# Where the block sums of the down projection's weights are made: 44 sums moved out of the SSD into the SSD output product and the mixing product

## The chip, the core and the metric

The kernel runs on one core of a Trainium2 chip. The metric is the time of one execution on the device, in microseconds (us). The engines are TensorE (PE; PEld are its weight loads), VectorE (DVE), ScalarE (ACT), GpSimd (POOL) and SyncE (SP), which here only issues DMA transfers. Each engine works through its own queue in order; an instruction that waits holds up what stands behind it.

## What is computed

A decoder layer over 1024 tokens of width 1024: two token mixers side by side (a Mamba-2 state-space mixer, SSD, and differential attention), merged by gates, followed by a gated feed-forward network with a convolution. Everything is float32. Cut to what matters:

```python
y_ssd = ssd_branch(z, xbc, dt_raw, ...)
y_att = diff_attention_branch(q, k, v, ...)
gate_ssd, gate_att = jnp.split(jax.nn.sigmoid(gates), 2, axis=-1)
merged = gate_ssd * (y_ssd @ w_ssd_o) + gate_att * (y_att @ w_attn_o)
mix = merged @ w_out
x = x + g1 * rms_norm(mix, post_norm1_w)
h2 = rms_norm(x, pre_norm2_w) * (1.0 + sc2) + sh2
u = causal_dwconv(h2 @ w_up, conv_ffn_w, conv_ffn_b)
u_gate, u_val = jnp.split(u, 2, axis=-1)
f = (jax.nn.gelu(u_gate, approximate=True) * u_val) @ w_down
x = x + g2 * rms_norm(f, post_norm2_w)
```

`w_down` is 2816 x 1024.

## The kernel before

**Products.** A float32 product is made of three passes in a faster format: each operand is split into a high part (a copy on ACT that rounds) and a low part (the difference, on DVE; helper `split`, L94 and L95), and high x high, high x low and low x high are summed in PSUM. The stages run one after another on PE: gates and convolved inputs, z, SSD, SSD output product, attention, merging, mixing product, up projection, down projection.

**The down projection** is computed with seven block products instead of eight (a Strassen-Winograd scheme), so it needs sums of the quarters of `w_down`. With KF = 11 blocks of rows k in each half, block k has the quarters b11, b12 (rows k) and b21, b22 (rows k + 11), each 128 x 512. Four sums per block are wanted: t1 = b12 - b11, t2 = b22 - t1, t3 = b22 - b12, t4 = b21 - t2. They depend on weights alone, so they can be made at any time before the down projection. They are made on DVE and stored in two DRAM tensors `wtd["12"]` and `wtd["34"]`, from which the down projection later loads them.

**Where they are made before.** In the SSD. `down_load` (L781) loads block k into one of two pairs of 512 KB buffers `wdr`; the generator `down_sums` (L786 to L794) makes one sum per turn into two extra buffers `wds`, and SP stores them, 512 KB for each two sums. The loop over u = 0 to 15 (8 chunks of 128 tokens, 2 groups of 8 heads) calls `sum_dn` at four places in each step, so that the 44 sums are spread over the steps u = 0 to 11 (none at 7).

**One step of the SSD.** `chunk_in(u + 1)` turns the next chunk's inputs on PE (px), copies them on ACT (xtk, L1070) and scales them on DVE (xd, L1073) and POOL; `chunk_decay` makes the decays M on ACT; `chunk_mask` multiplies them by the mask on DVE (L1092); `chunk_out(u)` forms po, the product of the state of before with C (L1099), which DVE reads into tt (L1100), and py, the product within the chunk (L1103), which DVE adds to y (L1105); `chunk_state(u)` forms the new state pst (L1117). po and pst use the one PSUM bank `wc` in turns. Between these, `fill` feeds PE with groups of three products of the attention's v (L1021 to L1023), whose weights are replaced once, at u = 7 (L1008 on ACT, L1009 on DVE, `fetch_v` on SP). The orders of PE, DVE, ACT and SP are as written here.

**The SSD output product** (j = 0 to 7) multiplies the turned SSD output by `w_ssd_o`: 48 products per step into one of two PSUM pairs, an evacuation with the gate on DVE (mout, L1324), a store of it on SP (msd, L1328). `fetch_seq(j + 6)` loads weights two steps ahead of their split, `split_seq(j + 5)` splits them one step ahead of use. At j = 0 the last block of q and k is rotated and stored (`rope`, `store_qk`), at j = 3 and 4 `load_qk` loads the q and k of the first heads of the attention. The order of SP is as written here too. The attention's first weights (w_q_raw, L1362; split at L1377 and L1374) and v tiles are loaded in this stretch as well, where the scheduler puts them.

**The mixing product** (i = 0 to 7, rows of 128 tokens) multiplies the merged mixers by `w_out` into two PSUM banks per row. `mix_square` (L1880) takes a row's squares on ACT; `mix_end(i)` ends the row, in this order on DVE: a sum of squares (L1884), a power on POOL (L1885), scaling and residual for two halves (L1895, L1896), their squares on ACT (L1897), the x1 store on SP (L1898), again L1884 and L1885, and the scaling L1900. `mix_end(i - 1)` is emitted within row i after its first quarter of products. Rows 2 and up take four PSUM banks in turns, so row i + 2 needs those of row i. In rows 5 and 6 `first_half` turns the finished rows 0 to 3 on PE (L1909) for the up projection, eight units through two PSUM banks, with two or three evacuations each on ACT (L1913, L1914, L1916) and a low part on DVE (L1917). PE, DVE, ACT and POOL run in the order written here; the scheduler orders SP.

**POOL's stores.** In the merging, `early_sums` (L1672 to L1678) already makes such sums, in place, for the up projection's first weights, and POOL issues their stores.

**Slots.** Buffers of 4 KB per partition come from a list of 43 (`Slots`): `get` takes the first free one, `put` appends it. Whoever gets a slot waits for its last user.

Of the kernel before, what the change touches and what calls it, by code (L numbers as in the profile page):

```python
# [11 lines left out]
F32 = mybir.dt.float32  # L12
F32R = mybir.dt.float32r
AF = mybir.ActivationFunctionType
ALU = mybir.AluOpType
AX = mybir.AxisListType

P = 128
D = 1024
S = 1024  # L20
HALF = 512
# [41 lines left out]
def kernel(ctx: ExitStack, tc: tile.TileContext, a: dict, out: bass.AP, dbg=None):  # L63
    nc = tc.nc
    V, A, G, T, SP = nc.vector, nc.scalar, nc.gpsimd, nc.tensor, nc.sync
# [15 lines left out]
    def ps_mm(name):  # L81
        return pmm.tile([P, 2, HALF], F32, tag="mm", name=name, bufs=2)
# [37 lines left out]
    def block_half(ps, w, x, half):  # L120
        mm3(ps, [((w[0][:, k, :], w[1][:, k, :]), (x[k][half][:, 0, :], x[k][half][:, 1, :])) for k in range(KD)])
# [302 lines left out]
    KF = NFF // 2  # L424
# [347 lines left out]
        SL.put(*evs_x, *cgv[(m - 1) % 2])  # L772


    dn_ops = deque()

    def down_load(k):
        if k < KF:
            for i in range(2):
                r0 = (k + KF * i) * P  # L780
                SP.dma_start(wdr[k % 2][i].rearrange("p h c -> p (h c)"), a["w_down"][r0 : r0 + P, :])  # L781

    def down_sums(k):
        (b11, b12), (b21, b22) = [(t[:, 0, :], t[:, 1, :]) for t in wdr[k % 2]]
        t1, t2, t3, t4 = wds[0][:, 0, :], wds[0][:, 1, :], wds[1][:, 0, :], wds[1][:, 1, :]
        V.tensor_tensor(t1, b12, b11, op=ALU.subtract)  # L786
        yield
        V.tensor_tensor(t2, b22, t1, op=ALU.subtract)
        SP.dma_start(wtd["12"][:, k, :, :], wds[0])
        yield  # L790
        V.tensor_tensor(t3, b22, b12, op=ALU.subtract)
        yield
        V.tensor_tensor(t4, b21, t2, op=ALU.subtract)
        SP.dma_start(wtd["34"][:, k, :, :], wds[1])  # L794
        down_load(k + 2)
        yield

    def all_sums():
        for k in range(KF):
            yield from down_sums(k)  # L800


    sm1 = SL.get("sm1", F32, (P, 8, 8, NH))
    sm2 = SL.get("sm2", F32, (P, 1024))
# [359 lines left out]
    for u in range(3):  # L1164
        load_decay(u)
    load_z(0)
    wdr = [[SL.get(f"wdr{i}{j}", F32, (P, 2, HALF)) for j in range(2)] for i in range(2)]
    wds = [SL.get(f"wds{i}", F32, (P, 2, HALF)) for i in range(2)]
    sums_dn = all_sums()

    def sum_dn(u, n):
        if u == 7 or (u == 8 and n < 2):
            return
        for _ in range(2 if u < 2 and n == 3 else 1):
            next(sums_dn, None)

    with tc.manual_schedule(engines={EN.PE, EN.DVE, EN.Activation, EN.SP}):
        for k in range(2):
            down_load(k)
        chunk_in(0)  # L1180
        fill(2)
        chunk_decay(0)
        chunk_mask(0, 0)
        chunk_mask(0, 1)
        lamt = const("lamt", [P, 2, 64])
        lams = const("lams", [P, 2])
        nlam = const("nlam", [P, 1])
        rl = rows[:, R_LAM : R_LAM + 256].rearrange("p (a b d) -> p a b d", a=2, b=2)
        V.tensor_tensor(lamt, rl[:, :, 0, :], rl[:, :, 1, :], op=ALU.mult)
        V.reduce_sum(lams, lamt, axis=AX.X)  # L1190
        A.activation(lams, lams, AF.Exp)
        V.tensor_tensor(nlam, lams[:, 1:2], lams[:, 0:1], op=ALU.subtract)
        V.tensor_scalar(nlam, nlam, -LAM_INIT, None, op0=ALU.add)
        subw = const("subw", [P, 1])
        V.tensor_scalar(subw, vec[:, V_SUB : V_SUB + 1], 1.0 - LAM_INIT, None, op0=ALU.mult)
        fill(4)
        for u in range(16):
            nxt = u + 1 < 16
            if u > 0:
                load_decay(u + 2)  # L1200
            if nxt:
                chunk_in(u + 1)
            fill(2)
            run_bg(2)
            sum_dn(u, 0)
            if nxt:
                chunk_decay(u + 1)
            run_bg(1)
            sum_dn(u, 1)
            if nxt:  # L1210
                chunk_mask(u + 1, 0)
            fill(2)
            chunk_out(u, (lambda: chunk_mask(u + 1, 1)) if nxt else (lambda: None))
            fill(3)
            run_bg(3)
            sum_dn(u, 2)
            chunk_state(u)
            fill(1 if u % 3 else 0)
            run_bg(1)
            sum_dn(u, 3)  # L1220
            if u % 2 == 1:
                chunk_norm(u // 2)
            if u == 11:
                assert next(sums_dn, None) is None
                SL.put(*wdr[0], *wdr[1], *wds)
                yr = [SL.get(f"yr{i}") for i in range(4)]
                ropc, rops = SL.get("ropc"), SL.get("rops")
                SP.dma_start(ropc, a["ropc"])
                SP.dma_start(rops, a["rops"])
                fetch_seq(0)  # L1230
                fetch_seq(1)
            elif u == 12:
                load_y(0)
        fill(16 * KD)
        run_bg(len(bg))
# [31 lines left out]
    def split_seq(n):  # L1267
        if n < len(seq):
            raw = seq_w[n]
            seq_w[n] = [wp.tile([P, KD, P], F32R, tag=f"w{x_}", name=f"{seq[n][0]}{seq[n][1]}_{x_}", bufs=4) for x_ in ("hi", "lo")]  # L1270
            split(*seq_w[n], raw)
# [11 lines left out]
    with tc.manual_schedule(engines={EN.PE, EN.DVE, EN.Activation, EN.SP}):  # L1283
        split_seq(0)
        old = None
        for n in range(4):
            fetch_seq(n + 2)
            ps = ps_mm(f"{seq[n][0]}p{seq[n][1]}")
            for half in range(2):
                block_half(ps[:, half, :], seq_w[n], hT, half)  # L1290
                if half == 0:
                    if old is not None:
                        rope(*old)
                    split_seq(n + 1)
                for k in turns[n][half]:
                    turn_y(k, n // 2)
                if n == 1 and half == 0:
                    load_y(1)
                if half == 0 and old is not None:
                    store_qk(*old[:2], hi, lo)  # L1300
            old = (*seq[n], ps)
        SL.put(*yr)


        gths = [SL.get(f"gth{i}") for i in range(2)]
        mouts = [SL.get(f"mout{i}") for i in range(2)]
        SP.dma_start(gths[0], gsd[0])
        for j in range(8):
            gth, mout = gths[j % 2], mouts[j % 2]
            fetch_seq(j + 6)  # L1310
            if j + 1 < 8:
                SP.dma_start(gths[(j + 1) % 2], gsd[j + 1])
            ps = ps_mm(f"so{j}")
            block_half(ps[:, 0, :], seq_w[j + 4], yT, 0)
            if j == 0:
                rope(*old)
                store_qk(*old[:2], hi, lo)
                SL.put(hi, lo, ropc, rops, qf, sw)
                qst, kst, klo = [[[SL.get(f"{n}0_{s}", F32R) for s in range(2)]] for n in ("qst", "kst", "klo")]
            split_seq(j + 5)  # L1320
            block_half(ps[:, 1, :], seq_w[j + 4], yT, 1)
            for half in range(2):
                hsl = slice(half * HALF, (half + 1) * HALF)
                V.scalar_tensor_tensor(mout[:, hsl], gth[:, hsl], 1.0, ps[:, half, :], op0=ALU.add, op1=ALU.mult)  # L1324
            if j in (3, 4):
                s = j - 3
                load_qk(s, qst[0][s], kst[0][s], klo[0][s])
            SP.dma_start(msd[j], mout)  # L1328
    SL.put(*gths, *mouts)
# [528 lines left out]
    rsm2 = const("rsm2", [P, 8])  # L1858
    pms = [None] * 8

    def load_res(i):
        SP.dma_start(xr[i], a["x"][i * P : (i + 1) * P, :])
        if i < 2:
            pms[i] = [(ps_wa, (ps_wb, ps_wc)[i])[ch](f"mix{i}_{ch}") for ch in range(2)]
        else:
            pms[i] = [ps_m(2 * (i % 2) + ch, f"mix{i}_{ch}") for ch in range(2)]
# [81 lines left out]
    with tc.manual_schedule(engines={EN.PE, EN.DVE, EN.Activation, EN.Pool}):  # L1948
        k0, k1 = range(KH), range(KH, KD)
        units = list(range(KD))  # L1950
        for i in range(8):
            if i == 0:
                for j in range(2):
                    load_res(j)
                for j in range(2):
                    mix_mms(j, 1, range(KD))
                for j in range(2):
                    mix_square(j, 1)
                mix_mms(0, 0, range(KD))
                mix_square(0, 0)  # L1960
                continue
            if i == 1:
                mix_mms(1, 0, k0)
                mix_end(0)
                mix_mms(1, 0, k1)
                mix_square(1, 0)
                continue
# [3 lines left out]
            for n, (ch, ks) in enumerate(((0, k0), (0, k1), (1, k0), (1, k1))):  # L1971
# [9 lines left out]
                    r1s = [SL.get(f"hr1{i}", F32, (P, 2, HALF)) for i in range(2)]  # L1981
                if n == 1:
                    mix_square(i, 0)
                if i in (5, 6):
                    for _ in range(1 + (i == 5 and n == 3)):
                        if units:
                            first_half(units.pop(0))
# [425 lines left out]
```

## Time and profile before

| | |
|---|---|
| median of 3 runs | 1841.29 us (1841.15 to 1841.5) |
| the profiled execution | 1841.71 us, its span 1839.9 us |
| mean granted clock of TensorE | 0.997 |
| PE busy | 1805.2 us, 98% |
| DVE busy | 1295.0 us, 70% |
| ACT busy | 896.3 us, 49% |
| POOL busy | 143.6 us, 8% |
| DMA | 334.66 MB, mean 182 GB/s |

The span runs from the first to the last instruction; the execution's time has the start and the end around it as well. Busy is the time in which an engine works on an instruction; the time in which it waits is not counted. In a row of the groups or of a timeline stand the line, the engine, the operation, out<-in by the program's names with their shapes, and in brackets how long the engine had been idle before it and what ended that. In the down stretch of the kernel nothing but loads of `wtd` (first at 1661.0 us of the span) uses the sums.

### The profile page before, as it was taken

The numbers are of one execution on the slowest core, as the hardware profiler recorded it, in microseconds if no ns is written. First come the engines' busy times: TensorE is split into PE (matmuls) and PEld (weight loads), VectorE is DVE, ScalarE is ACT, GpSimd is POOL, SyncE is SP. The second block draws the span as 40 slices with busy tenths as digits, with TensorE's granted clock in tenths as the row PEclk, the third lists the DMA queues.
The fourth block names the chain that finished last, engine by engine and source line by source line (L and its number), as shares of the span: only waits on it lengthen the run. The fifth ranks groups of instructions, "written<-read, shape, count | busy, mean of one in ns | idle before, by whom it ended". The sixth has DMA issues, their size and how long they took to land.

```text
span 1839.9 us, 24115 instructions
## 1 busy us (share of the span) xinstructions
PE 1805.2 (98%) x8787; PEld 1507.6 (82%) x8787; DVE 1295.0 (70%) x1978; ACT 896.3 (49%) x1744; POOL 143.6 (8%) x128
## 2 busy tenths in 40 slices
PE   7999999998999999999999999999999999999998
PEld 4888899876888888888888888888888888888887
DVE  7888877698753267767667563487998888876545
ACT  7554532545531046565567232565545454465532
POOL 0000000256420000000000100000000000000001
PEclk9999999999999999999999999999999999999999
DMA  9475367798747746676724764122333223379744
GB/s 374 180 246 172 99 206 265 263 358 303 281 128 208 228 124 172 173 192 159 192 87 160 240 209 157 57 87 100 112 109 109 103 97 109 108 233 309 247 154 162
DMA packets 133672, 334.66 MB, mean 182 GB/s; under 512 B 15009, under 2 KB 39345, under 8 KB 133554
## 3 DMA queue, kind: packets, MB, share of 16 engines
q1 hardware_dynamic: 132594, 329.98, 54.6%
q0 software_dynamic: 960, 3.15, 0.5%
q8 instruction: 69, 1.13, 0.3%
q14 instruction: 49, 0.40, 0.1%
HBM read 237.83 MB, written 95.23 MB: 181 GB/s over the span
## 4 chain that ended last, share of the span: by engine, by line
PE 65%; DVE 5%; ACT 3%; issue 1%; DMA 1%; POOL 0%; DVEq 0%; POOLq 0%; ACTq 0%
PE upx L1815 4%; PE upx L1816 4%; PE upx L1814 4%; PE o L1508 3%; PE upy L1815 2%; PE upy L1814 2%; PE upy L1816 2%; PE dx L2178 2%; PE dx L2179 2%; PE dx L2177 2%; PE at L1495 2%; PE dy L2178 2%; PE dy L2179 2%; PE dy L2177 2%; PE sc L1450 2%; PE ao L118 2%
## 5 line engine op out<-in xcount | busy, mean ns | idle before, releaser
L1814 PE MATMUL upx<-t,wu_t 128*128 128x512 f32 x264 | 103.2, 391 | 0.5 <-DVE cv L2242 0.4
L1815 PE MATMUL upx<-t,wu_t 128*128 128x512 f32 x264 | 102.8, 390 | 0.2 <-DVE t L1932 0.2
L1816 PE MATMUL upx<-t,wu_t 128*128 128x512 f32 x264 | 102.7, 389 | 0.0
L1788 ACT ACTIVATE wu_t<-sab 128x512 fp32r<-128x512 f32 x57 | 34.2, 627 | 128.3 <-DVE sab L1805 128.3
L1496 ACT COPY aT<-at 128x512 f32<-128x512 f32 (+2 forms) x96 | 46.1, 480 | 95.9 <-PE at L1495 95.9
L95 DVE TENSOR_TENSOR g_lo<-gst,g_hi 128x1024 fp32r<-128x1024 f32 (+1 forms) x42 | 47.6, 1135 | 50.7 <-ACT g_hi L94 50.6
L1508 PEld LDWEIGHTS o<-vt,aT 128*128 128x128 f32 x576 | 75.3, 191 | 9.2 <-ACT aT L1496 4.6
L1508 PE MATMUL o<-vt,aT 128*128 128x128 f32 x576 | 80.8, 276 | 0.4 <-ACT aT L1496 0.2
L94 ACT ACTIVATE g_hi<-gst 128x1024 fp32r<-128x1024 f32 (+1 forms) x42 | 41.6, 990 | 66.4 <-DMA gst<-gld_s 37.6
L1469 DVE TENSOR_REDUCE nmx<-sc 128x1 f32<-128x640 f32 (+3 forms) x64 | 65.6, 1025 | 2.2
L1449 PE MATMUL sc<-kst,qst 128*128 128x512 f32 (+2 forms) x192 | 63.7, 340 | 0.0
L1450 PE MATMUL sc<-klo,qst 128*128 128x512 f32 (+2 forms) x192 | 63.2, 346 | 0.0
L1832 DVE SCALAR_TENSOR_TENSOR ug<-cg,vec,ug 128x1023 f32<-128x1023 f32 (+1 forms) x44 | 56.3, 1280 | 6.1 <-ACT ug L1831 5.3
L1814 PEld LDWEIGHTS upx<-t,wu_t 128*128 128x128 f32 x264 | 49.5, 188 | 11.7 <-DVE cv L2242 1.3
L1815 PEld LDWEIGHTS upx<-t,wu_t 128*128 128x128 f32 x264 | 49.6, 188 | 10.7 <-DVE t L1932 0.5
L1792 DVE TENSOR_TENSOR wu_t<-sab,wu_t 128x512 fp32r<-128x512 f32 x57 | 39.3, 690 | 26.6 <-ACT wu_t L1788 26.6
L1816 PEld LDWEIGHTS upx<-t,wu_t 128*128 128x128 f32 x264 | 49.6, 188 | 10.3
L1832 DVE SCALAR_TENSOR_TENSOR uv<-cv,vec,uv 128x1023 f32<-128x1023 f32 (+1 forms) x44 | 56.2, 1278 | 0.9 <-ACT uv L1831 0.9
L1485 DVE RECIPROCAL rsm<-ssum 128x2 f32<-128x2 f32 x64 | 10.6, 166 | 62.6 <-ACT p L1482 35.4
L1487 DVE SCALAR_TENSOR_TENSOR p<-p,coef,p 128x128 f32<-128x128 f32 (+3 forms) x64 | 52.4, 819 | 2.3
L2298 POOL TENSOR_TENSOR rsf<-rsf,nhalf 128x1 f32<-128x1 f32 x8 | 5.3, 656 | 624.3 <-DVE rsf L2297 624.3
L2177 PE MATMUL dx<-wdt_hi,g_hi 128*128 128x512 f32 x132 | 51.3, 389 | 0.0
(546 smaller groups left out, 5871.0 us busy)
## 6 DMA issues: line engine op xcount, KB each, us to landing
adas<-in_w_ada SPq DMA_DIRECT2D x32, 512.0 KB, 4.8
wdr<-in_w_down SPq DMA_DIRECT2D x22, 512.0 KB, 6.8
wtd<-wds SPq DMA_DIRECT2D x22, 512.0 KB, 4.4
wuf<-in_w_up SPq DMA_DIRECT2D x22, 512.0 KB, 3.5
gld_s<-gsum SPq DMA_DIRECT2D x22, 512.0 KB, 2.8
gst<-gld_s SPq DMA_DIRECT2D x20, 512.0 KB, 4.6
wdt_raw<-wtd SPq DMA_DIRECT2D x20, 512.0 KB, 4.5
wuv<-in_w_up SPq DMA_DIRECT2D x19, 512.0 KB, 3.5
```

The source lines that it names most:

```text
L1449: T.matmul(sc[:, n0:n1], qs_[s][:, tsl], ks_[s][:, n0:n1], start=True, stop=False)
L1450: T.matmul(sc[:, n0:n1], qs_[s][:, tsl], kl[s][:, n0:n1], start=False, stop=True)
L1469: V.reduce_max(nmx[:, bq, s : s + 1], sc[:, :L], axis=AX.X, negate=True)
L1487: V.scalar_tensor_tensor(pr[0][:, :L], pr[1][:, :L], coef[:, bq : bq + 1], pr[0][:, :L], op0=ALU.mult, op1=ALU.add)
L1508: T.matmul(po_of[j, grp][:, qi, :], at[:, k, :], vt[j % 2][:, kt, :], start=(kt == 0), stop=(kt == i))
L1814: T.matmul(out_, wh, xh_, start=(k == 0 and first), stop=False, skip_group_check=not first)
L1815: T.matmul(out_, wh, xl_, start=False, stop=False, skip_group_check=not first)
L1816: T.matmul(out_, wl, xh_, start=False, stop=(k == end), skip_group_check=not first)
L1832: V.scalar_tensor_tensor(u[:, d:], c_[:, : S - d], fw[:, 2 - d : 3 - d], u[:, d:], op0=ALU.mult, op1=ALU.add)
L2177: T.matmul(o, gh[:, kk, tsl], wh, start=(k == 0 and not more), stop=False, skip_group_check=more)
L2178: T.matmul(o, gh[:, kk, tsl], wl, start=False, stop=False, skip_group_check=more)
L2179: T.matmul(o, gl[:, kk, tsl], wh, start=False, stop=(k == KF - 1), skip_group_check=more)
```

## The change

The sums leave the SSD. They are made in place, so `wds` is gone: t1 takes the place of b11, t3 that of b12, t2 that of b22, t4 that of b21, in the order t1, t3, t2, t4, and each is stored by itself (256 KB). Blocks 0 to 3 (16 sums) are made in the SSD output product: two blocks are loaded at j = 0 (two more at j = 2 and 3), and at j = 1 to 4 DVE makes four sums behind the split of that step, with SP issuing the stores. `load_qk` moves from j = 3 and 4 to j = 5 and 6, since its buffers are used for the blocks. Blocks 4 to 10 (28 sums) are made in the mixing product, with three pairs of buffers and POOL issuing the stores: 4 sums after row 0's products, 4 after `mix_end(0)`, and 7, 7 and 6 in rows 2, 3 and 4, behind the `mix_end` of the row before.

```diff
-    def down_sums(k):
-        (b11, b12), (b21, b22) = [(t[:, 0, :], t[:, 1, :]) for t in wdr[k % 2]]
-        t1, t2, t3, t4 = wds[0][:, 0, :], wds[0][:, 1, :], wds[1][:, 0, :], wds[1][:, 1, :]
-        V.tensor_tensor(t1, b12, b11, op=ALU.subtract)
...
-        SP.dma_start(wtd["34"][:, k, :, :], wds[1])
-        down_load(k + 2)
...
+    KSO = 4
+
+    def down_load(t, k, i):
+        r0 = (k + KF * i) * P
+        SP.dma_start(t[i].rearrange("p h c -> p (h c)"), a["w_down"][r0 : r0 + P, :])
+
+    def down_sum(t, k, n, q):
+        (b11, b12), (b21, b22) = [(x_[:, 0, :], x_[:, 1, :]) for x_ in t]
+        o, x_, y_ = ((b11, b12, b11), (b12, b22, b12), (b22, b22, b11), (b21, b21, b22))[n]
+        V.tensor_tensor(o, x_, y_, op=ALU.subtract)
+        q.dma_start(wtd[("12", "34", "12", "34")[n]][:, k, n // 2, :], o)
...
-        for k in range(2):
-            down_load(k)
         chunk_in(0)
...
-            sum_dn(u, 0)
...
-            sum_dn(u, 1)
...
-            sum_dn(u, 2)
...
-            sum_dn(u, 3)
...
             if u == 11:
-                assert next(sums_dn, None) is None
-                SL.put(*wdr[0], *wdr[1], *wds)
...
+            if 2 <= j < KSO:
+                for i in range(2):
+                    down_load(wdr[j % 2], j, i)
...
             if j == 0:
                 rope(*old)
                 store_qk(*old[:2], hi, lo)
-                SL.put(hi, lo, ropc, rops, qf, sw)
+                SL.put(ropc, rops, qf, sw, hi, lo)
+                wdr = [[SL.get(f"wdr{k}{i}", F32, (P, 2, HALF)) for i in range(2)] for k in range(2)]
+                for k in range(2):
+                    for i in range(2):
+                        down_load(wdr[k], k, i)
+            elif j == KSO + 1:
+                SL.put(*wdr[0], *wdr[1])
                 qst, kst, klo = [[[SL.get(f"{n}0_{s}", F32R) for s in range(2)]] for n in ("qst", "kst", "klo")]
             split_seq(j + 5)
+            if 1 <= j <= KSO:
+                for n in range(4):
+                    down_sum(wdr[(j - 1) % 2], j - 1, n, SP)
...
-            if j in (3, 4):
-                s = j - 3
+            if KSO < j < KSO + 3:
+                s = j - KSO - 1
                 load_qk(s, qst[0][s], kst[0][s], klo[0][s])
...
+    wdr = [[SL.get(f"wdm{k}{i}", F32, (P, 2, HALF)) for i in range(2)] for k in range(3)]
+    dn_todo = [(k, n) for k in range(KSO, KF) for n in range(4)]
+
+    def dn_step(count):
+        for _ in range(min(count, len(dn_todo))):
+            k, n = dn_todo.pop(0)
+            t = wdr[k % 3]
+            down_sum(t, k, n, G)
+            if n > 1 and k + 3 < KF:
+                down_load(t, k + 3, n - 2)
+            elif n == 3:
+                SL.put(*t)
...
             if i == 0:
                 for j in range(2):
                     load_res(j)
+                for k in range(KSO, KSO + 3):
+                    for n in range(2):
+                        down_load(wdr[k % 3], k, n)
...
                 mix_square(0, 0)
+                dn_step(4)
                 continue
             if i == 1:
                 mix_mms(1, 0, k0)
                 mix_end(0)
+                dn_step(4)
...
                 if n == 1:
                     mix_square(i, 0)
+                if n > 0 and i < 5:
+                    dn_step(3 if n < 3 else 1)
```

More of the change, by code (lines that the diff above doesn't have):

```diff
@@ L772 @@
         SL.put(*evs_x, *cgv[(m - 1) % 2])
[L775 to L781, printed above, removed]
-    def down_sums(k):
-        (b11, b12), (b21, b22) = [(t[:, 0, :], t[:, 1, :]) for t in wdr[k % 2]]
-        t1, t2, t3, t4 = wds[0][:, 0, :], wds[0][:, 1, :], wds[1][:, 0, :], wds[1][:, 1, :]
[L786 to L793, printed above, removed]
-        SP.dma_start(wtd["34"][:, k, :, :], wds[1])
-        down_load(k + 2)
[L796 to L800, printed above, removed]
+    KSO = 4
[7 more added lines that the diff above has]
+        q.dma_start(wtd[("12", "34", "12", "34")[n]][:, k, n // 2, :], o)
     sm1 = SL.get("sm1", F32, (P, 8, 8, NH))
@@ L1166 @@
     load_z(0)
[L1167 to L1175, printed above, removed]
     with tc.manual_schedule(engines={EN.PE, EN.DVE, EN.Activation, EN.SP}):
-        for k in range(2):
-            down_load(k)
         chunk_in(0)
```

## The prediction

> **What bounds the kernel now.** I read the busy times first, then the windows of the four stretches that the change touches: the SSD, the SSD output product, and the mixing product up to its fourth and in its last rows. The columns of a window are its bounds, its length, the busy time of PE, PEld, DVE, ACT and POOL with instruction counts, the granted clock, the DMA share and GB/s.
>
> ```profile
> PE 1805.2 (98%) x8787; PEld 1507.6 (82%) x8787; DVE 1295.0 (70%) x1978; ACT 896.3 (49%) x1744; POOL 143.6 (8%) x128
> ```
>
> ```profile
> 326.00:508.00 182.00, 171.76 (x889) 137.14 (x888) 146.60 (x209) 101.21 (x260) 89.37 (x64) 0.98 0.83 298
> 553.00:642.00 89.00, 88.88 (x396) 73.42 (x395) 27.33 (x35) 12.88 (x15) 3.43 (x1) 1.00 0.73 223
> 1107.00:1163.00 56.00, 56.00 (x249) 46.37 (x248) 20.49 (x35) 14.54 (x38) 4.38 (x8) 1.00 0.31 121
> 1163.00:1200.00 37.00, 36.71 (x178) 30.21 (x177) 21.01 (x36) 25.37 (x53) 3.26 (x6) 1.00 0.18 70
> ```
>
> PE sets the end: work taken off another engine is worth only the PE idle time that it causes. In all 1839.9 - 1805.2 = 34.7 us are idle, and the SSD holds 182.00 - 171.76 = 10.24 of them, beside a DVE busy 81% of the time and DMA at 0.83. The two places that receive the sums have a full PE and much DVE time free. So the question is how much of the 10.24 comes back, and whether the new places can hide 44 sums.
>
> The waits of PE inside the SSD, with total, times and longest:
>
> ```profile
> PE pst L1117 <- DVE tt L1100: 8.3, 5, 3.6
> PE v L1021 <- ACT wv_hi L1008: 1.2, 1, 1.2
> PE v L1022 <- DVE wv_lo L1009: 0.8, 1, 0.8
> ```
>
> They make 10.3, all of it. The state product (pst) shares one PSUM bank with po, and waits until DVE has read po into tt. The timelines of DVE and of PE around the longest wait say why tt is late; the last bracket is the idle time ahead and its releaser.
>
> ```profile
> 362.32 0.69 DVE L786 TENSOR_TENSOR wds<-wdr 128x512 f32<-128x512 f32 x1 [3.33 <-DMA wtd<-wds]
> ...
> 365.59 1.53 DVE L791 TENSOR_TENSOR wds<-wdr,wdr 128x512 f32<-128x512 f32 x1
> 367.04 0.68 DVE L793 TENSOR_TENSOR wds<-wdr,wds 128x512 f32<-128x512 f32 x1
> 367.64 0.68 DVE L1092 TENSOR_TENSOR M<-M,sm 128x512 f32<-128x512 f32 x1
> 368.25 0.68 DVE L1100 TENSOR_TENSOR tt<-po,sm 128x512 f32<-128x512 f32 x1
> ```
>
> ```profile
> 369.07 2.04 PE L1117 MATMUL pst<-xdd,sm 128*128 128x512 f32 x2 [3.56 <-DVE tt L1100]
> ...
> 374.96 0.42 PE L1021 MATMUL v<-wv_hi,hT 128*128 128x512 f32 x1
> ...
> 391.80 1.10 PE L1117 MATMUL pst<-xdd,sm 128*128 128x512 f32 x2 [0.76 <-DVE tt L1100]
> ...
> 394.90 0.39 PE L1021 MATMUL v<-wv_hi,hT 128*128 128x512 f32 x1
> ```
>
> A block sum stood 3.33 us at the head of DVE's queue for its own output buffer, and two more went ahead of tt. The same 15 instructions (pst to the third v group) then took 374.96 - 369.07 = 5.89 us after the long wait, 394.90 - 391.80 = 3.10 otherwise: 2.79 us lost again, at a reduced clock (the window's 0.98).
>
> **The change part by part.**
>
> *Removed from the SSD.* 44 sums on DVE, 22 loads and 22 stores on SP. The costliest and the cheapest of the four kinds, from the groups:
>
> ```profile
> L793 DVE TENSOR_TENSOR wds<-wdr,wds 128x512 f32<-128x512 f32 x11 | 13.9, 1266 | 0.0
> ...
> L786 DVE TENSOR_TENSOR wds<-wdr 128x512 f32<-128x512 f32 x11 | 8.5, 775 | 4.3 <-DMA wtd<-wds 4.3
> ```
>
> Each step of the loop loses about four sums, 3 to 5 us of DVE. The five tt waits are at most 3.56 us each with two or more sums ahead of tt in that step, so they go: -8.3. So does the slow clock, -2.8. The last pair, 1.2 + 0.8, is a weight load (wv_raw) issued only when DVE has finished a split; that split starts earlier and the load no longer shares DMA with 23 MB of sums, so I take -1.9, with zero as the other bound. Together **-13.0**, bounds -11.1 and -13.0. Nothing next in line is near: the loop's last steps have no sums and the window shows no PE wait there.
>
> *SSD output product: 16 sums in four steps, four 512 KB loads at once, then four more, 16 stores on SP.*
>
> ```profile
> 576.29 1.28 DVE L1324 SCALAR_TENSOR_TENSOR mout<-gth,so 128x512 f32<-128x512 f32 x2 [8.48 <-PE so L118]
> 578.50 1.23 DVE L95 TENSOR_TENSOR w_ssd_o_lo<-w_ssd_o_raw,w_ssd_o_hi 128x1024 fp32r<-128x1024 f32 x1 [0.93 <-ACT w_ssd_o_hi L94]
> 587.17 1.29 DVE L1324 SCALAR_TENSOR_TENSOR mout<-gth,so 128x512 f32<-128x512 f32 x2 [7.44 <-PE so L118]
> ```
>
> ```profile
> wdr<-in_w_down SPq DMA_DIRECT2D x22, 512.0 KB, 6.8
> wtd<-wds SPq DMA_DIRECT2D x22, 512.0 KB, 4.4
> ```
>
> ```profile
> 571.29 0.38 SPq L1328 DMA_DIRECT2D msd<-mout  x1
> ```
>
> A step lasts 587.17 - 576.29 = 10.88 us and DVE idles 7.4 to 8.5 of it, so four sums (2.7 at 0.68 each) fit. The tight place is step 1: behind the first waiting sum stand the evacuation (mout) and the split of the weights for step 3, and on SP behind the stores the next weight fetch. The loads go out where this first store of mout now stands on SP, at 571.3 to 573, and the first pair lands 6.8 later (the median of such loads, from the DMA issues), near 579; sums until 582, mout 583, split 585, needed at 587. Hidden by 2 us: **0**; if the loads take 10 it costs 1.5, and never below nothing, since PE is full.
>
> *Moved: the q/k loads of the first heads, two steps later.* Their ten issues go past the loads of the attention's first weights on SP.
>
> ```profile
> 623.85 0.38 SPq L1362 DMA_DIRECT2D w_q_raw<-in_w_q  x1
> ```
>
> ```profile
> 629.83 1.16 ACT L1377 ACTIVATE w_q_hi<-w_q_raw 128x512 fp32r<-128x512 f32 x2 [12.82 <-DMA w_q_raw<-in_w_q]
> ```
>
> ```profile
> 641.37 0.39 PE L1403 MATMUL w_qp<-hT,w_q_hi 128*128 128x512 f32 x1
> ```
>
> If the w_q load slips a whole step, its split starts at 629.83 + 10.88 = 640.7; high half 0.58, low half 0.69 give 642.0, plus 0.2 of handing over, where the third product wants it at 641.8. **+0.4**, bounds 0 and 2.
>
> *Mixing product: 28 sums on DVE between the row ends (4, 4, 7, 7, 6), each with a store that POOL issues, and the loads on SP.* Each row end (mix_end) is in order on DVE with two powers on POOL and two squares on ACT between; the first-half transposes stand behind it on ACT.
>
> ```profile
> 1125.28 0.16 DVE L1884 SCALAR_TENSOR_TENSOR rsm<-ssm 128x1 f32<-128x1 f32 x1 [11.12 <-ACT tm L1880]
> ...
> 1131.27 0.15 DVE L1884 SCALAR_TENSOR_TENSOR rsm<-ssm 128x1 f32<-128x1 f32 x1
> ...
> 1141.65 0.16 DVE L1884 SCALAR_TENSOR_TENSOR rsm<-ssm 128x1 f32<-128x1 f32 x1 [4.35 <-ACT tm L1880]
> ...
> 1163.41 0.16 DVE L1884 SCALAR_TENSOR_TENSOR rsm<-ssm 128x1 f32<-128x1 f32 x1 [4.83 <-ACT tm L1880]
> ```
>
> ```profile
> 1039.71 0.69 DVE L1673 TENSOR_TENSOR ws<-ws,ws 128x512 f32<-128x512 f32 x1
> 1040.44 0.69 DVE L1674 TENSOR_TENSOR ws<-ws,ws 128x512 f32<-128x512 f32 x1
> 1041.17 0.69 DVE L1675 TENSOR_TENSOR ws<-ws 128x512 f32<-128x512 f32 x1
> 1041.45 0.75 POOL L1677 DMA_DIRECT2D wsd<-ws  x1 [27.85 <-DVE ws L1674]
> ...
> 1052.31 0.54 POOL L1677 DMA_DIRECT2D wsd<-ws  x1 [8.49 <-DVE ws L1674]
> ```
>
> A row end holds DVE for 1131.27 - 1125.28 = 6.0 us, waits included, and a row lasts 10.9, so 4.35 to 4.83 are free. The early sums of the merging, also in place and stored through POOL, start 0.73 apart; I take 0.70. The last store (0.3 to start, 0.54 to issue) stands ahead of the next power, about 0.7 more per row end. So: the second row end starts at 1131.27 + 2.8 = 1134.1 (before: 1131.27); the third 6.0 + 0.7 + 4.9 later, 1145.7 (1141.65); the fourth 1157.3; the fifth, after six sums, 1157.3 + 6.0 + 0.7 + 4.2 = 1168.2 (1163.41), 4.8 late, and what hangs on its power 5.5 late. The PSUM banks of two rows on are needed later than that, but ACT is in order:
>
> ```profile
> 1169.08 0.68 ACT L1916 ACTIVATE hr<-h2tr,a2c 128x512 f32<-128x512 f32 x1
> ```
>
> ```profile
> 1171.57 0.60 PE L1909 MATMUL h2tr<-ident,xr 128*128 128x128 f32 x4
> ...
> 1174.76 1.03 PE L1909 MATMUL h2tr<-ident,xr 128*128 128x128 f32 x8
> ```
>
> The first transposed unit leaves its bank at 1169.08 + 0.68 = 1169.8, and PE's third unit wants it at 1171.57: 1.8 of slack against 5.5, so PE waits 3.7, and about 1 more at the fifth unit, directly behind the fourth. **+4.7**. With sums 0.61 apart, the spacing of unrelated ones above (367.04 to 367.64), and half the delay on POOL it is 1.1; with 0.75 and a full store, 6.3. It is not below nothing: PE has no idle time there to give.
>
> The loads need a look too. Seven blocks are 7.3 MB in and 7.3 MB out, 262 GB/s more over the 56 us, 383 beside the window's 121 at a share of 0.31: nearly all that DMA can do. So I use the landings under load, 6.8 and 4.4. A buffer comes round after three blocks. Block 9's load follows block 6's last stores (about 1144.5 + 4.4) and lands at 1155.7, where DVE wants it at 1155.3; block 10's second half lands at 1154 + 0.9 + 4.4 + 6.8 = 1166.1, wanted at 1166.1. Just in time; with a landing of 10 DVE stands about 3 more, which makes the upper bound 9.4. On SP, behind a load that waits for POOL's stores, stand only the x1 stores, which nobody waits for here.
>
> [...]
>
> *The sum.* The profiled execution took 1841.71 (span 1839.9 and 1.8 around it): 1841.71 - 13.0 + 0 + 0.4 + 4.7 = 1833.8. The median of the runs, 1841.29, is 0.4 below it: **1833.4**.
>
> **The rivals.** 1. *The mixing product hides everything* (lag under 1.8 us): 1841.3 - 13.0 = 1828.3. For it: PE is full there and DVE 37% busy; against: DVE's free 4.35 us per row are less than 4.9 + 0.7. 2. *The SSD gives back half*: another wait (ACT's M, POOL's yt) takes tt's place, so 6.5 returns, against 4.7 to 5.1: 1840. For it: ACT and POOL feed the same chain; against: the waits of PE name only sums' victims. 3. *Slower: POOL's queue becomes the bound.* Were a store beside sums to take s us, anything above the 0.70 between sums piles up ahead of the next power, for 24 stores. The gain of 13 is eaten when the lag reaches about 14, or 8.4 / 24 = 0.35 above 0.70: from s = 1.05. At 1.5 the lag is 5.5 + 24 x 0.8 = 25, the loss 24, the time 1852. For it: 0.75 once beside a sum; against: 0.54 the next time. 4. *The sums come too late for their reader*: the down projection, which reads them, comes after the whole up projection, so this has no weight.
>
> **How the numbers follow.** Forecast 58% (1830 to 1837.5), rival 1 16%, rival 2 14%, rival 3 12%. The range 1828 to 1840.5 takes in rivals 1 and 2 and the unfavourable bounds of the terms, all but rival 3. 0.2% is 3.7 us, about what a measurement of this kernel can tell from no change; faster by more means under 1837.6: forecast, rival 1 and a little of rival 2, 0.76; within it, most of rival 2, 0.11; slower, rival 3 and the tail of rival 2, 0.13.
>
> **What would show it.** Right: no wait of pst for tt in the SSD, PE idle there under 1 us and a clock of 1.00; in the mixing product row ends 3 to 5 us later against PE, and a PE wait of 3 to 5 us at the first-half transposes (L1909's counterpart) for ACT. POOL's stores near 0.55 to 0.75. Wrong: DVE standing in the mixing product for a load of the weights, a wait at the start of the attention above 2 us, or tt still late.

## The result, and the profile after

| | before | after |
|---|---|---|
| median of 9 runs each | 1840.27 us (eight of them 1839.55 to 1841.5) | 1845.66 us (1843.91 to 1846.93) |
| the profiled execution | 1841.71 us, its span 1839.9 us | 1846.93 us, its span 1845.1 us |
| ratio of after to before | | 1.0028 (95%: 1.0017 to 1.0038) |

One run of before took 2001.75 us and is not used in the ratio. The kernel became slower by about 5 us, where 8 us faster was forecast. PE works as long as before, so what was lost is again time in which it waits or runs at a lower clock:

```profile
PE 1805.5 (98%) x8787; PEld 1508.7 (82%) x8787; DVE 1293.2 (70%) x1978; ACT 895.1 (49%) x1744; POOL 147.8 (8%) x156
```

The windows of after, with the columns of the prediction's windows: the SSD, the SSD output product, the start of the attention, and the mixing product in two parts.

```profile
326.00:494.00 168.00, 167.82 (x892) 136.07 (x891) 116.78 (x166) 101.12 (x260) 78.12 (x64) 1.00 0.55 187
540.00:628.00 88.00, 87.70 (x389) 72.14 (x387) 35.59 (x46) 10.56 (x11) 3.43 (x1) 1.00 0.85 280
628.00:644.00 16.00, 5.66 (x14) 4.29 (x14) 3.87 (x6) 2.30 (x4) 0.00 (x0) 0.57 0.65 216
1107.00:1163.00 56.00, 56.00 (x249) 46.37 (x248) 33.17 (x56) 14.15 (x38) 15.99 (x29) 1.00 0.94 345
1163.00:1205.00 42.00, 38.06 (x176) 30.91 (x175) 25.61 (x43) 25.11 (x53) 6.58 (x12) 0.96 0.30 111
```

The SSD is now full: 0.2 us of PE idle in 168, at a clock of 1.00, where before it was 10.24 in 182 at 0.98. The SSD output product is full too, with DVE and DMA busier. But in the 16 us from 628 on PE works 5.66 us, at a clock of 0.57, and in the last rows of the mixing product it idles 4 us. The waits of PE name both:

```profile
PE w_qp L1381 <- ACT w_q_hi L1355: 10.3, 1, 10.3
PE h2tr L1900 <- ACT hr L1907: 3.7, 1, 3.7
...
PE so L118 <- DVE w_ssd_o_lo L95: 0.3, 1, 0.3
```

**The start of the attention.** SP's timeline of after, and what hung on it:

```profile
607.72 0.32 SPq L1306 DMA_DIRECT2D msd<-mout  x1
...
618.60 0.33 SPq L1306 DMA_DIRECT2D msd<-mout  x1
618.97 0.43 SPq L1406 DMA_DIRECT2D vt<-vd  x1
629.48 0.32 SPq L1306 DMA_DIRECT2D msd<-mout  x1
629.85 3.68 SPq L1406 DMA_DIRECT2D vt<-vd  x7
633.63 0.37 SPq L1340 DMA_DIRECT2D w_q_raw<-in_w_q  x1
```

```profile
637.79 1.15 ACT L1355 ACTIVATE w_q_hi<-w_q_raw 128x512 fp32r<-128x512 f32 x2 [34.29 <-DMA w_q_raw<-in_w_q]
638.47 0.80 PE L1381 MATMUL w_qp<-hT,w_q_hi 128*128 128x512 f32 x1 [10.34 <-ACT w_q_hi L1355]
...
643.33 0.59 PE L1383 MATMUL w_qp<-hT,w_q_lo 128*128 128x512 f32 x1
643.76 0.40 PE L1381 MATMUL w_qp<-hT,w_q_hi 128*128 128x512 f32 x1
```

After the store of mout of step 6 (618.60) SP issues one v tile, then stands for 10 us until step 7's mout is ready (629.48), then issues seven more v tiles, and only then w_q (633.63). Before, w_q stood behind the store of step 5. It has slid past two such stores, and two steps of 10.88 us less the 11.5 us between its split and PE's first product before (629.83 to 641.37) are 10.2, about the wait that is there. Behind it the twelve products from 638.47 to 643.76 take 5.29 us; at full clock products come 0.227 us apart (the pinned kernel below, at the same place, granted clock 1.00), which makes 2.72. So this place costs 10.34 + 2.57 = 12.9 us.

**The mixing product.** The starts of the second to fifth row end, one power's wait, and the third transposed unit with the fourth:

```profile
1133.69 0.15 DVE L1875 SCALAR_TENSOR_TENSOR rsm<-ssm 128x1 f32<-128x1 f32 x1
...
1145.31 0.15 DVE L1875 SCALAR_TENSOR_TENSOR rsm<-ssm 128x1 f32<-128x1 f32 x1
1146.96 0.75 DVE L1886 SCALAR_TENSOR_TENSOR tm<-mix,rsm,g1r 128x512 f32<-128x512 f32 x1 [1.50 <-POOL rsm L1876]
...
1156.81 0.15 DVE L1875 SCALAR_TENSOR_TENSOR rsm<-ssm 128x1 f32<-128x1 f32 x1
...
1167.77 0.15 DVE L1875 SCALAR_TENSOR_TENSOR rsm<-ssm 128x1 f32<-128x1 f32 x1
```

```profile
1175.01 0.66 PE L1900 MATMUL h2tr<-ident,xr 128*128 128x128 f32 x4 [3.65 <-ACT hr L1907]
...
1179.84 1.03 PE L1900 MATMUL h2tr<-ident,xr 128*128 128x128 f32 x8
```

Row ends, lag and wait are those of the forecast to within half a microsecond. From the first product of the mixing product to the first of the up projection it is 96.79 us (1107.66 to 1204.45), before 91.30 (1108.03 to 1199.33): 5.5 more, 3.65 of them the wait and 1.6 a slow clock behind it (the fourth unit comes 4.83 after the third, before 3.19).

The parts make up the whole: the first product of the SSD output product starts at 540.24 instead of 553.82, so the sum is 1841.71 - 13.6 + 0.3 + 12.9 + 5.5 = 1846.8, and the profiled execution took 1846.93.

### The profile page after: what moved, and what is told of

It reads as the page before. It is cut to its first block, busy times and chain, and to the rows that moved or that the text cites. A ratio compares the mean times of both kernels' runs of the same rounds, so it can differ in the third digit from the quotient of the medians.

```text
span 1845.1 us, 24178 instructions
## 1 busy us (share of the span) xinstructions
PE 1805.5 (98%) x8787; PEld 1508.7 (82%) x8787; DVE 1293.2 (70%) x1978; ACT 895.1 (49%) x1744; POOL 147.8 (8%) x156
## 4 chain that ended last, share of the span: by engine, by line
PE 82%; DVE 7%; ACT 3%; issue 3%; DMA 2%; POOL 1%; SPq 1%; POOLq 0%; DVEq 0%; ACTq 0%
PE upx L1793 4%; PE upx L1792 4%; PE upx L1794 4%; PE o L1486 3%; PE upy L1794 2%; PE upy L1792 2%; PE upy L1793 2%; PE dx L2176 2%; PE dx L2177 2%; PE dx L2175 2%; PE z L117 2%; PE z L118 2%; PE z L116 2%; PE dy L2175 2%; PE dy L2176 2%
## 5 line engine op out<-in xcount | busy, mean ns | idle before, releaser
L1794 PEld LDWEIGHTS upx<-t,wu_t 128*128 128x128 f32 x264 | 49.6, 188 | 10.3
L139 POOL TENSOR_TENSOR sqt<-sqt,nhalf 128x4 f32<-128x4 f32 x16 | 16.5, 1032 | 449.4 <-DVE sqt L138 449.4
```

The source lines that it names most:

```text
L1794: T.matmul(out_, wl, xh_, start=False, stop=(k == end), skip_group_check=not first)
```

## The experiments

The theory at this point: the SSD's loss was the sums' alone; the attention's start is late because of SP's order (transfers moved and added there push v and w_q behind two stores of mout), not because of busy DMA or a late buffer; the lag in the mixing product is DVE's sums and POOL's stores between the row ends.

### The SSD without any sums

```diff
@@ before @@
     def sum_dn(u, n):
-        if u == 7 or (u == 8 and n < 2):
-            return
-        for _ in range(2 if u < 2 and n == 3 else 1):
-            next(sums_dn, None)
+        return
...
-        for k in range(2):
-            down_load(k)
...
```

> Before, with the 44 sums, their loads and their stores left out of the SSD and made nowhere (the down projection reads quarters of the weights in their place, the same bytes); the q/k loads stay at steps 3 and 4. Theory (the SSD's loss is the sums' alone, 13.0 to 13.4): 1840.3 - 13.2 = 1827.1, no wait of pst for tt above 0.5, no wait at the start of the attention. Rival (another part of the chain takes tt's place as soon as the sums are gone): 1833 or more.

Measured: 1827.33 us (1826.84 to 1827.64), before 1839.92; ratio 0.9928 (0.9913 to 0.9943). The SSD's window reads as in after:

```profile
326.00:494.00 168.00, 167.81 (x890) 135.94 (x889) 116.88 (x165) 101.31 (x260) 77.25 (x64) 1.00 0.55 186
```

What the sums cost in the SSD is 12.6 us between medians, and after got all of it back there. This kernel is taken below as the floor for the versions that make the sums elsewhere.

### The start of the attention: five kernels

The q/k loads moved, nothing else:

```diff
@@ before @@
-            if j in (3, 4):
-                s = j - 3
+            if j in (5, 6):
+                s = j - 5
```

> Before, with only the q/k loads of the first heads moved from steps 3 and 4 to steps 5 and 6 of the SSD output product; the block sums stay in the SSD. Theory (the prediction's own step): the load of w_q slips by one step, behind the store of mout of step 6 but ahead of that of step 7, and PE waits 0 to 1 us: 1840.3 to 1841.3. Rival (the moved loads alone make the whole wait): w_q goes out behind the last store of mout, PE loses 10 to 13 us, 1850 to 1853.

Measured: 1840.32 us, ratio 1.0001 (0.9991 to 1.001). SP and ACT:

```profile
631.42 0.33 SPq L1328 DMA_DIRECT2D msd<-mout  x1
631.84 0.38 SPq L1362 DMA_DIRECT2D w_q_raw<-in_w_q  x1
...
642.30 0.32 SPq L1328 DMA_DIRECT2D msd<-mout  x1
```

```profile
637.26 1.16 ACT L1377 ACTIVATE w_q_hi<-w_q_raw 128x512 fp32r<-128x512 f32 x2 [21.29 <-DMA w_q_raw<-in_w_q]
```

The load slips by one step (623.85 to 631.84), the high part is done at 638.4 and PE takes its first product at 640.78 without a wait. So this edit alone does what the prediction said of it, and it is not the cause of the 10.3 us. The second step comes from something else that after does. (Here the v tiles go out early, behind the store of step 2, from 589.57.)

The 16 stores of the new sums taken off SP:

```diff
@@ after @@
-                    down_sum(wdr[(j - 1) % 2], j - 1, n, SP)
+                    down_sum(wdr[(j - 1) % 2], j - 1, n, G)
```

> After, with POOL instead of SP issuing the 16 stores of the SSD output product's sums. Theory (the 16 stores on SP push the v loads, and with them w_q, behind one more store of mout): v goes out by step 4, w_q behind the store of mout of step 6 only, PE waits 0 to 1 us at the start of the attention: 1845.7 - 12.5 = 1833.2. Rivals (the buffer that v takes over from a block, or busy DMA, is the cause): the wait of 10.3 stays, 1845.7.

Measured: 1834.96 us (1832.65 to 1836.95), ratio to before 0.9969 (0.9959 to 0.9979). SP:

```profile
597.91 3.65 SPq L1406 DMA_DIRECT2D vt<-vd  x8
601.66 0.38 SPq L1306 DMA_DIRECT2D msd<-mout  x1
...
618.67 0.33 SPq L1306 DMA_DIRECT2D msd<-mout  x1
619.10 0.38 SPq L1340 DMA_DIRECT2D w_q_raw<-in_w_q  x1
```

With the stores on POOL, v goes out ahead of the store of step 4 and w_q behind that of step 6; no wait of w_qp is left among PE's waits. The bytes are the same, and in the window from 540 to 628 DMA is even busier (0.90 against 0.85 in after), so busy DMA isn't the cause; SP's list is. The choice of issuer was worth 10.7 us between the medians: in after, SP stands from 619.4 to 629.48 for step 7's mout, with seven v tiles and w_q behind that store.

The rival that blames the buffer (v takes one that a block had):

```diff
@@ after @@
                 SL.put(*wdr[0], *wdr[1])
+                vt_0 = SL.get("vt0", F32, (P, 8, P))
...
```

> After, with the attention's first v tile put into a buffer that no block of weights used. Theory (SP's order, set by how many transfers stand on SP, not by the buffer): the order stays, the wait of w_qp at the start of the attention stays at 10.3, 1845.7. Rival (v, and w_q behind it, wait for the store of a block out of the buffer that v takes over): v goes out before the last two stores of mout, the wait falls under 1 us, 1832.6.

Measured, one run: 1846.08 us, no better than after. Its trace has the order of after (one v tile, the last store of mout, seven v tiles, w_q at 633.49) and a wait of 10.5 us. The buffer is not the cause.

Another order of emission, the place left to the scheduler:

```diff
@@ after @@
     def dense_stream():
-        fetch(0)
-        fetch(1)
...
+    fetch(0)
+    fetch(1)
     load_heads(0)
```

> After, with the loads of w_q and w_k emitted ahead of those of v, their place on SP left to the scheduler. Theory (w_q is late because it stands behind the eight v loads, which themselves went behind the last store of mout): w_q goes out behind the store of mout of step 6, PE waits 0 to 1 us: 1833. Rival (the place is set by SP's load alone, whatever the order of emission): w_q stays behind the last store of mout, at 630 instead of 633.6, the wait falls to about 6, 1841.

Measured: 1835.88 us (1834.1 to 1837.41), ratio 0.9975 (0.9966 to 0.9985). w_q goes out at 619.05 and its high part is ready at 624.7, but one wait stays, half a microsecond longer than expected:

```profile
PE w_qp L1381 <- DVE w_q_lo L1352: 1.5, 1, 1.5
```

```profile
627.88 1.28 DVE L1302 SCALAR_TENSOR_TENSOR mout<-gth,so 128x512 f32<-128x512 f32 x2 [9.60 <-PE so L118]
629.08 1.29 DVE L1352 TENSOR_TENSOR w_q_lo<-w_q_raw,w_q_hi 128x512 fp32r<-128x512 f32 x2
```

DVE idles 9.60 us and then runs the last evacuation ahead of the low part, though the raw weights had landed by 623.57, when ACT began with them. It is the same fault one queue on: an order that no data requires.

Pinned, in SP's fixed order:

```diff
@@ after @@
+            if j == 6:
+                fetch(0)
+                fetch(1)
             ps = ps_mm(f"so{j}")
...
     def dense_stream():
-        fetch(0)
-        fetch(1)
```

> After, with the loads of the attention's first two weights (w_q, w_k) written into SP's fixed order at step 6 of the SSD output product. Theory (SP's order alone makes the 10.3 us wait): the loads go out at about 608 us, the wait of w_qp for w_q_hi is under 1 us, the attention's first products run at full clock, and the time is 1845.7 - 13.1 = 1832.6 (0.996 of before). Rival (DMA is too busy there, share 0.85): the loads land late all the same, a wait above 5 us stays, 1840 or more.

Measured: 1833.75 us (1832.23 to 1834.61), ratio 0.9966 (0.9953 to 0.9979).

```profile
608.10 0.81 SPq L1257 DMA_DIRECT2D w_q_raw<-in_w_q  x1
```

The load goes out 25 us earlier and the wait is gone; at the top of PE's waits now stands the third transposed unit's, 3.6 us.

### The mixing product: five kernels

Without its 28 sums:

```diff
@@ after @@
-    dn_todo = [(k, n) for k in range(KSO, KF) for n in range(4)]
+    dn_todo = []
...
```

> After, without the 28 sums of the mixing product, their loads and their stores (left out; the down projection reads the sums of blocks 0 to 3 again in their place, the same bytes). Theory (DVE's row ends and POOL's powers behind the stores are late by the sums): row ends as before, no wait of the third first-half unit for ACT, the wait at the start of the attention stays at 10.3: 1845.7 - 5.4 = 1840.3. Rival (the late unit is a result of the shift in the attention): the wait of 3.7 stays, 1845.7.

Measured: 1840.14 us (1839.44 to 1841.09), 5.5 below after; ratio to before 1.0001 (0.9991 to 1.001). No wait of the third unit is left, while that of w_qp stays at 10.0. With w_q and w_k pinned it was the other way round. The two losses are independent of each other.

DVE or POOL? On the pinned kernel, SP issues the stores:

```diff
@@ pinned @@
-            down_sum(t, k, n, G)
+            down_sum(t, k, n, SP)
```

> The pinned version, with SP instead of POOL issuing the 28 stores of the mixing product's sums. Theory (part of the lag is the last store on POOL ahead of each row end's first power, 1.5 us instead of 0.65): the power's wait falls to 0.65, the fifth row end comes about 2 us late instead of 4.7, the wait of the third first-half unit falls from 3.6 to at most 0.6: 1829. Rival (DVE's sums alone make the lag): the wait stays above 3, 1833.8. Other rival (SP falls behind with the loads): DVE stands for loads, slower than 1833.8.

Measured: four runs of 1828.14, 1828.53, 1833.27 and 1834.05 us; median 1830.9, ratio 0.9949 (0.9933 to 0.9964). The profile is that of the slowest:

```profile
1131.20 0.15 DVE L1877 SCALAR_TENSOR_TENSOR rsm<-ssm 128x1 f32<-128x1 f32 x1
1132.00 0.75 DVE L1888 SCALAR_TENSOR_TENSOR tm<-mix,rsm,g1r 128x512 f32<-128x512 f32 x1 [0.65 <-POOL rsm L1878]
...
1141.90 0.15 DVE L1877 SCALAR_TENSOR_TENSOR rsm<-ssm 128x1 f32<-128x1 f32 x1
...
1152.97 1.42 DVE L784 TENSOR_TENSOR wdm<-wdm,wdm 128x512 f32<-128x512 f32 x2 [3.11 <-DMA wdm<-in_w_down]
...
1155.04 0.15 DVE L1877 SCALAR_TENSOR_TENSOR rsm<-ssm 128x1 f32<-128x1 f32 x1
```

```profile
1161.42 1.11 PE L1902 MATMUL h2tr<-ident,xr 128*128 128x128 f32 x4 [3.34 <-ACT hr L1909]
```

The theory shows, and so does the second rival's stand for loads. The power's wait is 0.65 again, and the third and fourth row ends are 10.7 us apart instead of 11.5, so the 0.85 us per row was POOL's. But then DVE stands 3.11 us for the load of a block, the fifth row end comes 5.3 us later than before instead of about 2, and PE's wait at the third unit is 3.34, not the 0.6 expected: in this execution the gain is lost again. Whether SP fell behind is not shown: DVE stands for a load in the next kernel too, where POOL issues the stores. That the two faster runs are those in which the load came in time is likely, but not shown: they have no profile.

Sums put where DVE waits anyway inside a row end:

```diff
@@ pinned @@
         rstd_row(i, ssm)
+        gap()
         between()
...
         SP.dma_start(x1d[i], tm)
+        gap()
         rstd_row(i, ssx)
+        gap()
```

(gap() makes one sum; 2 to 4 sums per row stay behind the row end.)

> The pinned version (w_q and w_k written into step 6), and in the mixing product three sums of each row end put where DVE waits inside the row end: behind the issue of each power, and ahead of the second sum of squares; the rest (2 to 4) behind the row end. Theory (DVE's row ends are late because its sums fill more than the free time between row ends): row ends no more than 2 us late, no wait of the third first-half unit: 1833.8 - 5.4 = 1828.4. Rival (POOL's stores ahead of the powers are the cause, wherever the sums stand): a wait of 2 to 4 us stays, 1832 to 1834.

Measured: 1828.38 us (1827.79 to 1828.93), ratio 0.9934 (0.9918 to 0.9951). One row end of it:

```profile
1134.50 0.16 DVE L1877 SCALAR_TENSOR_TENSOR rsm<-ssx 128x1 f32<-128x1 f32 x1 [0.18 <-ACT xr L1891]
1134.58 0.69 DVE L784 TENSOR_TENSOR wdm<-wdm,wdm 128x512 f32<-128x512 f32 x1
1135.88 0.76 DVE L1896 TENSOR_SCALAR xr<-tm,rsm 128x1024 f32<-128x1024 f32 x1 [0.61 <-POOL rsm L1878]
...
1140.36 0.69 DVE L784 TENSOR_TENSOR wdm<-wdm,wdm 128x512 f32<-128x512 f32 x1 [2.37 <-DMA wdm<-in_w_down]
```

The wait for ACT's squares falls from 0.79 to 0.18, since a sum fills it. The sum beside the power is no full gain: DVE waits 0.61 behind it all the same, and the scaling starts 1.38 after the sum of squares instead of 0.82. On POOL the store of the sum that fills ACT's wait stands ahead of the power, from 1134.72 for 0.54 us. Counted from the first product of the mixing product, the second to fifth row ends come 2.2, 1.9, 2.8 and 1.4 us later than before (in after 2.8, 4.0, 4.7 and 4.7), so the 2 us expected was passed twice. PE waits 0.3 and 0.6 at the transposes. What is left is again a load: 2.37 us at 1140.

The same kernel beside the one without sums, on one chip:

> The version with w_q and w_k pinned and the sums in the gaps of the row ends, once more, beside the kernel that makes no sums at all. Theory (both new places now hide the sums): within 2 us of that kernel, 1828.4. Rival (44 sums cost DMA or DVE time that PE still pays for): 3 us or more above it.

Measured: 1829.07 us (1827.35 to 1831.71), ratio 0.9939 (0.9924 to 0.9954), against 1827.33 without any sums: 1.7 above the floor. In the execution profiled this time the same sum stood 3.29 us for its load, and PE waited 2.0 at the third unit.

A fourth pair of buffers:

```diff
@@ sums in the gaps @@
-    wdr = [[SL.get(f"wdm{k}{i}", F32, (P, 2, HALF)) for i in range(2)] for k in range(3)]
+    wdr = [[SL.get(f"wdm{k}{i}", F32, (P, 2, HALF)) for i in range(2)] for k in range(4)]
...
-            if n > 1 and k + 3 < KF:
-                down_load(t, k + 3, n - 2)
+            if n > 1 and k + 4 < KF:
+                down_load(t, k + 4, n - 2)
...
```

> The version with w_q and w_k pinned and the sums in the gaps of the row ends, with four pairs of buffers for the mixing product's blocks instead of three. Theory (what is left of the lag is DVE standing 2.4 to 3.3 us for a block's load that waits for its buffer): that wait goes, the third first-half unit waits under 0.5, 1828.0, with less spread than the 1827.4 to 1831.7 of three pairs. Rival (DMA itself is full, share 0.84 to 1.03 from 1093 to 1150 us, so an earlier load only moves the queue): DVE stands for a load at another place, time and spread as with three pairs.

Measured: 1828.96 us (1827.24 to 1829.12), ratio 0.9937 (0.9923 to 0.995). DVE's waits for loads in this stretch, and the window that was short of a load before:

```profile
DVE wdm L784 <- DMA wdm<-in_w_down: 0.6, 1, 0.6
```

```profile
1130.00:1140.00 10.00, 10.00 (x46) 8.29 (x45) 8.21 (x16) 2.71 (x8) 5.28 (x9) 1.00 1.03 418
```

The long load wait is gone, though DMA is as full as with three pairs (1.03 and 411 GB/s in the same ten microseconds). So DMA's rate was enough; the load had started too late, because its buffer came round late. From the mixing product's first product to the up projection's it is 91.33 us in this profile, as in before (91.30). The time is the same as with three pairs within the measurement; the slowest run is 1829.1 instead of 1831.7, with too few runs to call that shown. Either version is 11 to 12 us below before.

## Why the prediction was wrong, point by point

**The SSD, -13.0: right.** It gave 13.6 between the traces, and the kernel without sums gave 12.6 between medians. The rival in which another wait takes tt's place is out: the window holds 0.2 us of idle PE. The 2.8 of slow clock in that sum belongs to the profiled execution of before. In that of the q/k move alone, whose SSD is the same, the longest wait for tt was 2.88 us and nothing was lost behind it (last section), so this term is not there in every execution.

**The SSD output product, 0: right,** with 0.3.

**The q/k loads' move, +0.4 with 2 as its upper bound: this is the step that failed.** It cost 12.9. The prediction put it thus: the ten issues go past the loads of the attention's first weights, and "if the w_q load slips a whole step" PE waits 0.4. The move alone does just that and costs nothing. What failed is the premise that one step was the most it could slip. The prediction counted on SP only the ten moved issues, and charged the 16 new stores only for what stands behind them in the fixed order. They also push the v tiles, which stand ahead of w_q: with the 16 stores on SP these went out behind the stores of mout of steps 6 and 7, without them ahead of that of step 4, and w_q took its second step with them. It had 11.5 us from its split to PE's first product, one step and 0.7, of which the high half takes 0.6, so the second step came out nearly whole, 10.34, and the clock behind the wait cost 2.6 more. The profile of before held the warning; v, ahead of w_q on SP, already went out in two parts around a store of mout:

```profile
612.66 2.32 SPq L1428 DMA_DIRECT2D vt<-vd  x5
621.12 0.32 SPq L1328 DMA_DIRECT2D msd<-mout  x1
...
621.96 1.80 SPq L1428 DMA_DIRECT2D vt<-vd  x3
```

The upper bound of 2 had no row behind it; two steps less the slack, 10.2 without the clock, was the bound to write down.

**The mixing product, +4.7: right in mechanism and nearly in size,** 5.5. Row ends came within 0.5 us of those worked out, and the wait at the third unit was 3.65 where 3.7 stood. The fifth unit's wait of about 1 did not come; a slow clock of 1.6 behind the wait was there instead, though the prediction had read the same effect in the SSD. That 4.7 came so near to 5.5 is in part luck: one term that was not there stood in for another that was left out. Its two halves, DVE's overrun and POOL's last store, are both shown by the runs. The upper bound's warning, loads just in time, did not come true in after, but did as soon as the row ends came earlier.

**The rivals.** None named the place that decided, although "a wait at the start of the attention above 2 us" stood among the signs of a wrong prediction. POOL's queue didn't become the bound: its 28 stores in after took 0.54 to 0.58 us each, where the third rival needed 1.05 or more.

**What stays open:** why the scheduler places the v tiles behind step 7's store. The runs show that the 16 stores off SP bring them forward, with the moved q/k loads kept, and that another buffer doesn't, not the scheduler's reason. Nor do they show what decides whether a wait brings the slow clock.

## What to carry to other kernels

When an edit adds or moves transfers on a queue whose order is partly written out and partly chosen by a scheduler, bound a load's slip by whole steps of the written order, compare with its slack, and write the load into the order if two steps would hurt. Sums that are to hide on an engine hid better here in waits that its chain had anyway than behind it (1828.4 us against 1833.8); then look at the buffers that feed them. Waits of 2.0 to 10.3 us on a full PE cost here 1.6 to 2.8 us more than their own length, by the clock behind them, and one of 2.9 us nothing more, so put that into the range.

## What the runs showed of the hardware

**The clock behind a wait.** Behind PE waits of 2.00 us (second run of the sums in the gaps), 3.34 (SP's stores), 3.65 and 10.34 us (both in after) products came 0.43 us apart instead of 0.227, for 3 to 6 us (a granted clock of 0.50 in the 6.2 us behind the wait of 3.34), and 1.6, 2.8, 1.6 and 2.6 us were lost on top. Behind waits of 0.28 us (first run of the sums in the gaps) and 1.53 us (the loads emitted first) they came 0.23 us apart and nothing was lost. Length alone does not decide: behind a wait of 2.88 us in the SSD of the q/k move alone the granted clock was 1.00 and nothing was lost, in the place where before's 3.56 us lost 2.8. The waits of 2.00 and 2.88, and the window behind the second:

```profile
1159.53 0.66 PE L1905 MATMUL h2tr<-ident,xr 128*128 128x128 f32 x4 [2.00 <-ACT hr L1912]
```

```profile
369.29 1.10 PE L1117 MATMUL pst<-xdd,sm 128*128 128x512 f32 x2 [2.88 <-DVE tt L1100]
```

```profile
369.30:375.00 5.70, 5.70 (x26) 4.32 (x27) 5.10 (x9) 3.04 (x9) 3.87 (x3) 1.00 0.93 341
```

After the wait of 3.65 us the first products still came 0.23 apart, and the slow ones began 1 us later:

```profile
1175.73 0.40 PE L1867 MATMUL mix<-wo_lo,mT 128*128 128x512 f32 x1
1175.96 0.39 PE L1868 MATMUL mix<-wo_hi,mT 128*128 128x512 f32 x1
...
1176.58 0.63 PE L1867 MATMUL mix<-wo_lo,mT 128*128 128x512 f32 x1
```

**POOL's stores beside DVE.** In the version with the sums in the gaps, the stores on POOL that fell beside the scaling of a row (L1896, TENSOR_SCALAR, 0.75 us) took 0.95 to 0.96 us, four of them, at 1117.09, 1125.67, 1135.80 and 1147.58; beside sums and elsewhere they took 0.54 to 0.59.

**DMA.** In the version with four pairs DMA ran at a share of 0.90 to 1.03 from 1093 to 1150 us, with up to 418 GB/s (the window above), and PE worked without a pause and at a clock of 1.00 beside it.
